# Two rounds of three chains in the first mixer of a two-block transformer kernel, with products in runs, and the modulation vectors computed in another stage

## The chip, the cores and the metric

The kernel runs on one core of a Trainium2 chip. The metric is the device time of one execution in microseconds (us), from runs on the chip. TensorE (PE in the profile) does the matrix products, VectorE (DVE), ScalarE (ACT) and GpSimd (POOL) the work on elements, and SyncE (SP) issues the transfers from memory. Each engine has one instruction queue, worked through in order.

## The reference

Two blocks follow each other, on one sequence of 256 positions with 1024 features, all in fp32.

```python
def first_block(x, p, ...):                 # two layers
    for i in range(2):
        h = rmsnorm(x, norm_mix_g[i])
        if i == 0:
            proj = h @ even_w_in[0]
            y_a = rwkv7_group(h, ...)        # 8 heads of 64: a recurrence over positions
            y_b = gdn_group(...)             # 4 heads of 128: the gated delta rule
            mix = concat(y_a, y_b) @ even_w_out[0]
        else:
            mix = chunk_band_attention(h, ...) @ attn_w_out[0]
        x = x + mix
        x = x + square(relu(rmsnorm(x) @ mlp_w1[i])) @ mlp_w2[i]
        x = x + rmsnorm(p[i] @ ple_w_proj[i]) * sigmoid(x @ ple_w_gate[i])
    return x

def second_block(x, c, ctx, c_ctx, w_ada, b_ada, ...):
    for layer in range(2):
        mod_l = silu(c) @ w_ada[layer] + b_ada[layer]      # w_ada[layer] is [1024, 6144]
        mod_c = silu(c_ctx) @ w_ada[layer] + b_ada[layer]
        # shifts, scales and gates of both streams come from mod_l and mod_c
        ...
```

## The kernel before

**Weights and products.** The activations lie with features on partitions, as eight tiles of 128 features by 256 positions. For fp32 accuracy each matrix product is done as three: weights and activations are split into a high and a low part. A weight piece [128, 1024] (512 KB, tile raw) is loaded by SP; ACT makes its high part (tile hi), and an engine named by `k.weng` makes the low part as raw - hi (tile lo); pools of four raw, three hi and three lo buffers hold them. `mm3` then issues the three products of a 128 x 128 block. Such products, 128 x 128 by 256 columns, are called dense below.

**The order.** The code is traced into instructions with a priority each, and a scheduler puts them in a fixed order per engine before the kernel runs. `k.at(p)` sets the priority of what is traced next (smaller is earlier), and `k.spread(p0, p1, n)` spreads the pieces of a dense chunk evenly over a stretch of priorities. The order is therefore decided by numbers in the code, not at run time.

**The first mixer** (`layer0_mixer`). The RWKV7 heads make four units and the gated delta rule (GDN) two; each unit is a chain of small steps for two heads: products of 64 x 64 or 128 x 64 on PE, each followed by DVE or ACT, which feed the next product. In both kinds there is the inverse of a triangular matrix by doubling (`triangular_inverse`: tiles Tt, Tg, Pg, Aa). Six units run in three rounds of two: RWKV units 0 and 1, RWKV units 2 and 3, GDN units 0 and 1. A round has `UNIT` = 320 priorities, both of its units start at the same one, and each unit has a lane: its own work buffers and two PSUM banks (`k.lane`, pools psX0 to psX2; psD is for dense products, psG for the modulation vectors). Between the small products stand dense ones, which need no unit: chunks 3, 1, 5 of the input projection w_ein in the first round, chunks 6, 8, 10, 7, 9, 11 and the gates of GDN (`gdn_gates`) in the second, chunks 12, 13, the RWKV half of the output projection (`out_proj1`) and the projection of the PLE gate (`ple[0].products`) in the third.

**The modulation vectors** of block 2's first layer (`ada`) are computed in the mixer too: a loop over 12 chunks of 512 columns, each with 4 pieces of 512 KB (tile adaraw) and 8 products of 32 result rows by 512 columns. Four column groups of PE (q = 0, 32, 64, 96) each take a quarter of the work; ACT copies the result (adat), four transposes and a sum on DVE bring it into place. The chunks lie `STEP` = 65 priorities apart. Those of the second layer are computed later in block 2, on DVE (`ada_sums`).

**What follows the mixer**: `out_proj`, the MLP of layer 0 (`mlp`, whose second half reads tile hh), the PLE gate, and `layer1_mixer`, the banded attention with its projection w_qkv, then the same again for layer 1, and block 2.

While the first mixer runs, `k.weng` is GpSimd; everywhere else, and in the mixer's first two chunks, it is DVE.

Of the kernel before, what the change touches and what calls it, by code (L numbers as in the profile page):

```python
# [19 lines left out]
P = 128  # L20
# [171 lines left out]
def layout(i):  # L192
# [22 lines left out]
    A["w_ada0"] = pack_w(i["w_ada_2"][0], 2, 512)  # L215
# [19 lines left out]
STEP = 65  # L235
F10 = 12
F20 = 7
# [3 lines left out]
OFS0 = 140  # L241
# [31 lines left out]
class K:  # L273
    def __init__(self, nc, tc, A, es):
        self.nc, self.tc, self.A, self.es = nc, tc, A, es
        self.cp = self.pool("const", 1)
        self.wraw = self.pool("wraw", 4)
        self.whi = self.pool("whi", 3)
        self.wlo = self.pool("wlo", 3)
        self.psG = self.pool("psG", 1, PSUM)  # L280
# [4 lines left out]
        self.weng = nc.vector  # L285
        self.slots = None
        self.later, self.slow = [], []
# [85 lines left out]
    def mm(self, out, lhsT, rhs, start=True, stop=True):  # L373
        self.nc.tensor.matmul(out=out, lhsT=lhsT, rhs=rhs, start=start, stop=stop)  # L374

    def tr(self, out, in_):
        self.nc.tensor.transpose(out=out, in_=in_, identity=self.ident)  # L377
# [410 lines left out]
def gdn_gates(k, gp, hgl, wbb, rb):  # L788
# [6 lines left out]
    ps = k.psX.tile([P, 2, T], F32, name="psx")  # L795
# [4 lines left out]
    ps = k.psX.tile([P, 2, 8], F32, name="psx")  # L800
# [18 lines left out]
    psn = k.psX.tile([P, 512], F32, name="psx")  # L819
# [151 lines left out]
def layer0_mixer(k, x, bg, ple):  # L971
# [5 lines left out]
    f1ps = [k.pool(f"f1{i}", n, es=es) for i, n in enumerate((F10, L1, L1))]  # L977
    f2ps = [k.pool(f"f2{i}", n, es=es) for i, n in enumerate((F20, L2, L2))]
# [10 lines left out]
    lanes = [lane(1), lane(2)]  # L989
# [72 lines left out]
    bg()  # L1062
    lo2 = []
    weng, k.weng = k.weng, nc.vector
# [3 lines left out]
    k.weng = weng  # L1068
# [47 lines left out]
    for q in range(3):  # L1116
        p = t0 + q * L
        if q == 0:
            dense((3, 1, 5), evac_rkv, p, p + L * 0.9)
        elif q == 1:  # L1120
            dense((6, 8, 10, 7, 9, 11), evac_gdn, p, p + L)
            k.at(p + L // 2)
            G = gdn_gates(k, gp, H, wbb, rb)
        else:
            dense((12, 13), evac_gdn, p, p + L * 0.5)
            yh, yl = y = k.acts(0)
            for m in range(4):
                k.split_act(yh[:, m, :T], yl[:, m, :T], ya[m])
            with k.spread(p + EO[0] * L, p + EO[1] * L, 16):
                for _ in out_proj1(k, "w_eout", y, x, [(0, 0, 4)]):  # L1130
                    pass
            k.at(p + PL * L)
            for _ in ple.products(lambda: k.psD.tile([P, 2, T], F32, name="psx")):
                pass
        for u in range(2):
            k.at(p + u * OFS)
            k.lane(1 + u)
            if q < 2:
                m = 2 * q + u
                ya.append(rwkv_unit(k, m, rkv[0, m], rkv[1, m], rkv[2, m], lt, lo2, rst, *lanes[u]))  # L1140
            else:
                yo.append(gdn_unit(k, u, G, [kq[2 * u], kq[2 * u + 1]], raws[1, u], raws[2, u], *lanes[u]))
            k.lane(0)
    k.at(t0 + 3 * L)
# [209 lines left out]
def layer1_mixer(k, xg, r, pass1):  # L1354
# [46 lines left out]
    pipe, groups = Pipe(), []  # L1401
    for g in range(4):
# [29 lines left out]
def ada(k, l, es, step, ofs=0):  # L1432
# [3 lines left out]
    w = k.pool("adaw", 2 if l else 3, es=es, side="right")  # L1436
# [8 lines left out]
    for c in range(12):  # L1445
        k.tc.cur_priority = p + step * c
        ps = k.psG.tile([P, 512], F32, name="psg")
        for pi in range(4):
            raw = w.tile([P, 2, 512], F32, name="adaraw")
            nc.sync.dma_start(out=raw, in_=k.A[f"w_ada{l}"][c, pi].rearrange("p (j n) -> p j n", j=2))  # L1450
            for j in range(2):
                kk = 2 * pi + j
                q = 32 * (kk % 4)
                nc.tensor.matmul(out=ps[q:q + 32], lhsT=sv[:, kk], rhs=raw[:, j], start=kk < 4, stop=kk >= 4, tile_position=(0, q))  # L1454
# [759 lines left out]
def program(nc, tc, A, out):  # L2214
    with ExitStack() as es:
# [4 lines left out]
        es1 = ExitStack()  # L2220
        k.plep = k.pool("plep", 1, es=es1, side="right")
        ple = [Ple(k, l) for l in range(2)]
        with ExitStack() as esa:
# [7 lines left out]
        for l in range(2):  # L2231
            st = k.stat_begin(stp, "ffn")
            xg = k.acts(1)
            out_proj(k, "w_eout" if l == 0 else "w_ao", y, x, f"gffn{l}", st, xg, [(1, 2, 2)] if l else [(1, 0, 4)])
# [7 lines left out]
            mlp(k, l, x, xg, st, xs, ple[l].norm, context if l else None)  # L2242
            if l == 0:
# [8 lines left out]
                y = layer1_mixer(k, nx, r, lambda y: chain(out_proj1(k, "w_ao", y, x, [(0, 0, 4), (1, 0, 2)]), ple[1].products(lambda: k.psD.tile([P, 2, T], F32, name="psx"))))  # L2252
# [23 lines left out]
```

## Time and profile before

| | us |
|---|---|
| median of 3 runs | 1981.81 |
| lowest and highest run | 1980.93, 1985.22 |
| the profiled execution, its own time | 1984.02 |
| its span, from the first to the last instruction | 1982.2 |
| PE busy in it | 1904.9 |
| DVE, ACT, POOL busy | 1382.6, 911.6, 161.3 |

The profiled execution is 2.2 us above the median, and 1.8 us of its time lie outside the span. Busy times are those of a hardware profiler; a matmul's end is modelled, and an fp32 matmul leaves two records where the instruction is one (for the small products and those of the modulation vectors). Of TensorE's clock the profile shows the granted share: 1.00 is 2.4 GHz and 0.50 is 1.2 GHz.

In time, the mixer's three rounds lie at about 68 to 175, 175 to 301 and 301 to 389 us; the first product of the second half of layer 0's MLP starts at 494.3 us; the attention lies at about 608 to 729 us.

### The profile page before, as it was taken

Reading aid. Unit: us, or ns where it says so; the run is one execution under the profiler, and the core shown is the slowest. Engines: PE = TensorE matmul, PEld = TensorE weight load, DVE = VectorE, ACT = ScalarE, POOL = GpSimd, SP = SyncE. Lnnn points to the kernel's source line nnn. Section 1 sums busy time; section 2 is a strip of 40 time slices with the busy share of each in tenths; the row PEclk is TensorE's granted clock in tenths of the full one; section 3 lists DMA queues with packets and bytes.
Section 4 is the critical chain, followed back from the end, with each engine's and each line's share of the span. In section 5 each row is a group of like instructions: output and inputs, shape, how many; then the busy total and the mean of one; then the engine's idle time right before and its main releaser. Section 6 shows DMA issues by size and latency. Waiting matters only on the chain.

```text
span 1982.2 us, 36281 instructions
## 1 busy us (share of the span) xinstructions
PE 1904.9 (96%) x14540; PEld 1682.0 (85%) x14540; DVE 1382.6 (70%) x2838; ACT 911.6 (46%) x1527; POOL 161.3 (8%) x211
## 2 busy tenths in 40 slices
PE   7999999999999999999999998899999999899998
PEld 4665668899999889999998887678888898788998
DVE  6544627586558878676876789859877578888664
ACT  4313224455446665545465555433213354465443
POOL 3412214100000100000001100000000000200000
PEclk9999978999999999999999999899999999999999
DMA  6544312255655446556422113235774254324553
GB/s 242 205 165 149 97 57 75 67 186 184 194 192 199 154 130 206 185 193 195 154 81 62 44 38 104 90 128 197 239 267 157 86 172 158 107 77 161 189 182 127
DMA packets 84401, 292.14 MB, mean 147 GB/s; under 512 B 9639, under 2 KB 11528, under 8 KB 83976
## 3 DMA queue, kind: packets, MB, share of 16 engines
q1 hardware_dynamic: 84232, 289.82, 44.3%
q8 instruction: 114, 1.87, 0.4%
q14 instruction: 55, 0.45, 0.1%
HBM read 288.73 MB, written 1.05 MB: 146 GB/s over the span
## 4 chain that ended last, share of the span: by engine, by line
PE 81%; DVE 13%; ACT 2%; issue 2%; POOL 1%; DMA 0%; ACTq 0%; SPq 0%; DVEq 0%
PE psx L374 75%; PE psg L1454 3%; DVE lo L364 3%; PE psx L377 2%; PE psg L374 1%; ACT hi L361 1%; POOL qb L364 1%; DVE mt L371 1%; DVE act L371 0%; DVE qx L364 0%; DVE hu L371 0%; ACT act L361 0%; DVE qms L1309 0%; DVE act L364 0%; DVE nt L364 0%
## 5 line engine op out<-in xcount | busy, mean ns | idle before, releaser
L374 PE MATMUL psx<-act,hi 128*128 128x256 f32 (+1 forms) x3872 | 830.2, 309 | 23.4 <-ACT hi L361 11.4
L361 ACT ACTIVATE hi<-raw 128x1024 fp32r<-128x1024 f32 (+1 forms) x440 | 453.6, 1032 | 652.0 <-PE psx L374 459.1
L374 PEld LDWEIGHTS psx<-act,hi 128*128 128x128 f32 x3872 | 633.9, 192 | 92.3 <-issue 32.4
L364 DVE TENSOR_TENSOR lo<-raw,hi 128x1024 fp32r<-128x1024 f32 (+1 forms) x406 | 482.0, 1189 | 265.8 <-ACT hi L361 264.2
L374 PE MATMUL psx<-act,lo 128*128 128x256 f32 (+1 forms) x1936 | 596.4, 308 | 4.1 <-DVE lo L364 3.6
L374 PEld LDWEIGHTS psx<-act,lo 128*128 128x128 f32 x1936 | 371.7, 192 | 42.1 <-issue 18.8
L374 PE MATMUL psx<-hi,act 128*128 128x256 f32 x1280 | 242.2, 289 | 2.7 <-ACT act L361 1.5
L374 PEld LDWEIGHTS psx<-hi,act 128*128 128x128 f32 x1280 | 198.8, 190 | 11.2 <-issue 7.0
L374 PE MATMUL psx<-lo,act 128*128 128x256 f32 x640 | 180.8, 283 | 1.2 <-DVE lo L364 1.2
L374 PE MATMUL psx<-fh,hi 128*128 128x256 f32 (+2 forms) x528 | 162.3, 308 | 4.9 <-DVE xc L371 4.9
L374 PE MATMUL psx<-fh,lo 128*128 128x256 f32 (+2 forms) x528 | 162.4, 308 | 1.3 <-DVE lo L364 1.3
L374 PE MATMUL psx<-fl,hi 128*128 128x256 f32 (+2 forms) x528 | 161.7, 306 | 0.0
L374 PE MATMUL psx<-hh,hi 128*128 128x256 f32 x512 | 142.4, 278 | 0.0
L374 PE MATMUL psx<-hlo,hi 128*128 128x256 f32 x512 | 142.2, 278 | 0.0
L374 PE MATMUL psx<-hh,lo 128*128 128x256 f32 x512 | 142.2, 278 | 0.0
L374 PEld LDWEIGHTS psx<-lo,act 128*128 128x128 f32 x640 | 121.5, 190 | 1.4 <-DVE lo L364 1.4
L374 PEld LDWEIGHTS psx<-fh,hi 128*128 128x128 f32 x528 | 101.3, 192 | 10.9 <-issue 6.0
L374 PEld LDWEIGHTS psx<-fh,lo 128*128 128x128 f32 x528 | 101.3, 192 | 8.0 <-DVE lo L364 2.1
L374 PEld LDWEIGHTS psx<-fl,hi 128*128 128x128 f32 x528 | 101.3, 192 | 4.5
L364 POOL TENSOR_TENSOR lo<-raw,hi 128x1024 fp32r<-128x1024 f32 x34 | 81.4, 2396 | 223.6 <-ACT hi L361 167.7
L1484 DVE CUSTOM_DVE_ANT_0 adat<-adaraw,adac 128x1024 f32<-128x1024 f32 x64 | 78.3, 1223 | 28.1 <-DMA adaraw<-in_w_ada 27.1
L374 PEld LDWEIGHTS psx<-hlo,hi 128*128 128x128 f32 x512 | 96.9, 189 | 0.0
(499 smaller groups left out, 2501.6 us busy)
## 6 DMA issues: line engine op xcount, KB each, us to landing
raw<-in_w_m SPq DMA_DIRECT2D x128, 512.0 KB, 3.4
adaraw<-in_w_ada SPq DMA_DIRECT2D x96, 512.0 KB, 4.2
raw<-in_w_up SPq DMA_DIRECT2D x92, 512.0 KB, 3.3
raw<-in_w_dn SPq DMA_DIRECT2D x48, 512.0 KB, 3.4
raw<-in_w_ein SPq DMA_DIRECT2D x28, 512.0 KB, 4.7
raw<-in_w_ie SPq DMA_DIRECT2D x28, 512.0 KB, 3.4
raw<-in_w_qkv SPq DMA_DIRECT2D x24, 512.0 KB, 3.5
raw<-in_w_io SPq DMA_DIRECT2D x18, 512.0 KB, 3.7
```

What stands on the lines that cost most here:

```text
L361: self.nc.scalar.activation(out=out, in_=in_, func=func, **kw)
L364: (eng or self.nc.vector).tensor_tensor(out=out, in0=a, in1=b, op=op)
L371: (eng or self.nc.vector).scalar_tensor_tensor(out=out, in0=a, scalar=s, in1=b, op0=op0, op1=op1)
L374: self.nc.tensor.matmul(out=out, lhsT=lhsT, rhs=rhs, start=start, stop=stop)
L377: self.nc.tensor.transpose(out=out, in_=in_, identity=self.ident)
L1454: nc.tensor.matmul(out=ps[q:q + 32], lhsT=sv[:, kk], rhs=raw[:, j], start=kk < 4, stop=kk >= 4, tile_position=(0, q))
L1484: nc.vector.tensor_tensor_reduce(out=t, in0=raw, in1=row[:, s], scale=1.0, scalar=0.0, op0=ALU.mult, op1=ALU.add, accum_out=mod[:, j, s:s ...
```

## The change

The six units run in two rounds of three (RWKV 0, 1, 2; then RWKV 3, GDN 0, 1), with a third lane of buffers and banks; psG, the bank of the modulation vectors, is opened after the mixer only. Chunks 3, 1, 5 stand in the first quarter of the first round, then the gates (with their products in the dense banks psD), then chunks 6 to 11. The products that a unit traces directly behind each other are kept together (`k.chains`, `k.pe`): the first of such a run keeps its priority, the others get priority 0 with the condition to be issued after the first. `ada` is called in the attention, with 2 pieces of 1 MB a chunk, each with four products in a run, and `STEP` = 120. The low part of a weight is made by DVE everywhere. The PLE projection of layer 0 stands in its MLP, and the fourth piece of the output projection's RWKV half in `out_proj`.

```diff
-STEP = 65
+STEP = 120
-F20 = 7
+F20 = 10
-OFS0 = 140
+OFS0 = 100
...
-        self.nc.tensor.matmul(out=out, lhsT=lhsT, rhs=rhs, start=start, stop=stop)
+        self.pe(lambda: self.nc.tensor.matmul(out=out, lhsT=lhsT, rhs=rhs, start=start, stop=stop))
...
+    def pe(self, emit):
+
+        if not self.runs:
+            emit()
+            return
+        traced = self.nc.cur_bb.bb.instructions
+        if self.head is not None and traced[-1] is self.last:
+            p = self.now
+            self.at(0)
+            with self.tc.issue_after(self.head):
+                self.last = emit().ins
+            self.at(p)
+        else:
+            self.head = self.last = emit().ins
...
-        self.tt(lo[:, :n], raw[:, :n], hi[:, :n].bitcast(F32), ALU.subtract, eng=self.weng)
+        self.tt(lo[:, :n], raw[:, :n], hi[:, :n].bitcast(F32), ALU.subtract)
...
-    ps = k.psX.tile([P, 2, T], F32, name="psx")
+    ps = k.psD.tile([P, 2, T], F32, name="psx")
...
-    k.banks(2, 1, 2, 2)
+    k.banks(2, 2, 2, 2)
...
-    for q in range(3):
+    rwkv = lambda u, m: ya.append(rwkv_unit(k, m, rkv[0, m], rkv[1, m], rkv[2, m], lt, lo2, rst, *lanes[u]))
+    gdn = lambda u, i: yo.append(gdn_unit(k, i, G, [kq[2 * i], kq[2 * i + 1]], raws[1, i], raws[2, i], *lanes[u]))
+    for q in range(2):
         p = t0 + q * L
         if q == 0:
-            dense((3, 1, 5), evac_rkv, p, p + L * 0.9)
-        elif q == 1:
-            dense((6, 8, 10, 7, 9, 11), evac_gdn, p, p + L)
-            k.at(p + L // 2)
+            dense((3, 1, 5), evac_rkv, p, p + L * 0.25)
+            k.at(p + L * 0.25)
             G = gdn_gates(k, gp, H, wbb, rb)
+            dense((6, 8, 10, 7, 9, 11), evac_gdn, p + L * 0.25, p + L)
+            units = [(rwkv, 0), (rwkv, 1), (rwkv, 2)]
         else:
             dense((12, 13), evac_gdn, p, p + L * 0.5)
...
-                for _ in out_proj1(k, "w_eout", y, x, [(0, 0, 4)]):
+                for _ in out_proj1(k, "w_eout", y, x, [(0, 0, 3)]):
                     pass
-            k.at(p + PL * L)
-            for _ in ple.products(lambda: k.psD.tile([P, 2, T], F32, name="psx")):
-                pass
-        for u in range(2):
+            units = [(rwkv, 3), (gdn, 0), (gdn, 1)]
+        for u, (f, i) in enumerate(units):
             k.at(p + u * OFS)
-            k.lane(1 + u)
...
+            k.lane(u)
+            with k.chains():
+                f(u, i)
...
-        for pi in range(4):
-            raw = w.tile([P, 2, 512], F32, name="adaraw")
...
+        for pi in range(2):
+            raw = w.tile([P, 4, 512], F32, name="adaraw")
+            nc.sync.dma_start(out=raw, in_=k.A[f"w_ada{l}"][c, pi].rearrange("p (j n) -> p j n", j=4))
+
+            with k.chains():
+                for j in range(4):
+                    q = 32 * j
+                    k.pe(lambda: nc.tensor.matmul(out=ps[q:q + 32], lhsT=sv[:, 4 * pi + j], rhs=raw[:, j], start=pi == 0, stop=pi == 1, tile_position=(0, q)))
...
-            k.weng = nc.gpsimd
-            y = layer0_mixer(k, x, lambda: ada(k, 0, esa, STEP, OFS0), ple[0])
-            k.weng = nc.vector
...
+                y = layer1_mixer(k, nx, r, lambda y: chain(out_proj1(k, "w_ao", y, x, [(0, 0, 4), (1, 0, 2)]), ple[1].products(space)), lambda: ada(k, 0, esm, STEP, OFS0))
```

The order of PE before, in the first inverse of the first round (each row is a run of equal instructions; Tg, Aa, Pg, Tt are the inverse's tiles, adaraw and sv the modulation's weights and vector, act with hi or lo a dense product):

```order
L374 MATMUL psx<-Tg,Aa 64x64 x16
L1454 MATMUL psg<-adaraw,sv 32x512
L374 MATMUL psx<-Pg,Tt 64x64 x16
L1454 MATMUL psg<-adaraw,sv 32x512 x4
L374 MATMUL psx<-Tg,Aa 64x64 x16
L1454 MATMUL psg<-adaraw,sv 32x512
L374 MATMUL psx<-act,lo 128x256
L374 MATMUL psx<-act,hi 128x256 x2
L374 MATMUL psx<-act,lo 128x256
L374 MATMUL psx<-Pg,Tt 64x64 x16
```

Two units' steps take turns there with modulation products, alone or in fours, and with single dense ones. The same place after (bbrow belongs to the gates):

```order
L373 MATMUL psx<-tm,Aa 64x64 x24
L822 MATMUL psx<-ct,bbrow 128x8 x2
L373 MATMUL psx<-Tg,Aa 64x64 x24
L373 MATMUL psx<-Pg,Tt 64x64 x24
...
L373 MATMUL psx<-Tt,Pg 64x64 x24
L373 MATMUL psx<-Tt,tm 64x64 x24
L373 MATMUL psx<-Z,Tt 64x64 x24
L373 MATMUL psx<-tm 128x128
```

Each step is now a run of 24 products of three units, and nothing else stands between the steps: the dense products of chunks 6 to 11 come behind the inverse. PE after, in the attention, where before there are dense products alone (hi and lo with act are those of w_qkv, adat the copied result that is transposed):

```order
L373 MATMUL psx<-hi,act 128x256 x2
L1471 MATMUL psg<-adaraw,sv 32x512 x4
L373 MATMUL psx<-lo,act 128x256
L373 MATMUL psx<-hi,act 128x256
L1471 MATMUL psg<-adaraw,sv 32x512 x4
L373 MATMUL psx<-hi,act 128x256
L373 MATMUL psx<-lo,act 128x256
...
L376 MATMUL psg<-ct,adat 128x128 x4
```

All modulation products have moved there, in 24 groups of four (three chunks have both of their groups behind each other), with twelve groups of four transposes. Behind the MLP of layer 1 the order of PE is the same in both kernels.

## Rows read from the trace of the kernel before

**Rows 1.** The page: span, and PE's busy time, share and instructions.
```profile
span 1982.2 us, 36281 instructions
PE 1904.9 (96%) x14540; PEld 1682.0 (85%) x14540; DVE 1382.6 (70%) x2838; ACT 911.6 (46%) x1527; POOL 161.3 (8%) x211
```

**Rows 2.** Windows: stretch, length, each engine's busy time, clock, DMA share, GB/s.
```profile
0.00:494.30 494.30, 465.53 (x3994) 359.46 (x3995) 286.04 (x610) 193.93 (x321) 106.08 (x86) 0.95 0.42 143
68.00:175.00 107.00, 100.29 (x944) 65.12 (x947) 56.11 (x149) 30.30 (x63) 24.57 (x22) 0.97 0.47 161
175.00:301.00 126.00, 122.01 (x976) 78.58 (x968) 57.79 (x167) 38.30 (x77) 23.98 (x19) 0.87 0.29 95
301.00:389.00 88.00, 83.50 (x906) 75.32 (x904) 57.94 (x147) 39.46 (x67) 31.25 (x21) 0.95 0.21 67
414.50:494.30 79.80, 79.80 (x674) 79.78 (x673) 57.63 (x74) 43.84 (x57) 0.00 (x0) 1.00 0.57 188
608.00:729.00 121.00, 118.25 (x993) 110.06 (x992) 92.54 (x293) 74.50 (x164) 8.64 (x4) 0.99 0.47 155
```

**Rows 3.** PE's groups by operation, 0 to 389 us: busy, mean ns, idle before.
```profile
L374 PE MATMUL psx<-act,hi 128*128 128x256 f32 x576 | 134.7, 315 | 12.1 <-ACT hi L361 10.9 <-DVE zsh L364 1.2
...
L1454 PE MATMUL psg<-adaraw,sv 128*32 128x512 f32 x192 | 76.2, 616 | 1.9 <-DMA adaraw<-in_w_ada 1.9
...
L377 PE MATMUL psg<-ct,adat 128*128 128x128 f32 x48 | 9.0, 295 | 0.0
```

**Rows 4.** PE's timeline from 60 us: start, duration, instruction.
```profile
60.54 0.28 PE L374 MATMUL psx<-act,lo 128*128 128x256 f32 x1
60.65 0.28 PE L374 MATMUL psx<-act,hi 128*128 128x256 f32 x1
60.87 1.05 PE L1454 MATMUL psg<-adaraw,sv 128*32 128x512 f32 x4
61.85 0.39 PE L374 MATMUL psx<-act,hi 128*128 128x256 f32 x1
62.07 0.28 PE L374 MATMUL psx<-act,lo 128*128 128x256 f32 x1
```

**Rows 5.** PE's timeline from 113 us, in the first inverse.
```profile
113.34 1.04 PE L1454 MATMUL psg<-adaraw,sv 128*32 128x512 f32 x2
114.32 1.20 PE L374 MATMUL psx<-Pg,Tt 64*64 64x64 f32 x32
115.45 1.06 PE L1454 MATMUL psg<-adaraw,sv 128*32 128x512 f32 x8
```

**Rows 6.** Windows of five stretches at the low clock, 104 to 323 us.
```profile
104.40:111.30 6.90, 6.90 (x52) 5.69 (x51) 1.11 (x5) 1.26 (x3) 0.00 (x0) 0.51 0.45 167
...
248.20:272.10 23.90, 23.90 (x84) 16.24 (x84) 5.09 (x21) 9.04 (x17) 2.43 (x2) 0.51 0.13 45
...
sum 47.80, PE 47.41 PEld 34.35 DVE 13.60 ACT 14.64 POOL 5.60; mean PE 9.48 PEld 6.87 DVE 2.72 ACT 2.93 POOL 1.12
```

**Rows 7.** ACT's and DVE's timeline in the same inverse.
```profile
113.41 0.66 ACT L361 ACTIVATE Pg<-psx 128x256 f32<-128x256 f32 x2
115.52 0.79 DVE L619 COPY_PREDICATED Tg<-cm,psx 128x256 f32<-128x256 uint32 x2 [5.49 <-PE psx L374]
116.19 0.76 DVE L634 STREAM_TRANSPOSE Tt<-Tg 128x256 f32<-128x256 f32 x2
```

**Rows 8.** Window of a stage in block 2, columns as in Rows 2.
```profile
1200.00:1300.00 100.00, 84.81 (x463) 71.14 (x462) 85.14 (x207) 50.11 (x101) 0.78 (x10) 0.88 0.29 95
```

**Rows 9.** Groups of POOL and DVE up to 480 us: the low parts.
```profile
L364 POOL TENSOR_TENSOR lo<-raw,hi 128x1024 fp32r<-128x1024 f32 x34 | 81.4, 2396 | 223.6 <-ACT hi L361 167.7 <-PE psx L374 29.4 <-ACT Pg L361 26.4
...
L364 DVE TENSOR_TENSOR lo<-raw,hi 128x1024 fp32r<-128x1024 f32 x35 | 42.7, 1223 | 19.0 <-ACT hi L361 18.8
```

**Rows 10.** The page: transfer rate in 40 slices, and the main queue's MB and share.
```profile
GB/s 242 205 165 149 97 57 75 67 186 184 194 192 199 154 130 206 185 193 195 154 81 62 44 38 104 90 128 197 239 267 157 86 172 158 107 77 161 189 182 127
...
q1 hardware_dynamic: 84232, 289.82, 44.3%
```

More of the change, by code (lines that the diff above doesn't have):

```diff
@@ L284, in __init__ @@
         self.pse = None
-        self.weng = nc.vector
         self.slots = None
+        self.runs, self.head = False, None
         self.later, self.slow = [], []
@@ L373, in mm, with chains @@
     def mm(self, out, lhsT, rhs, start=True, stop=True):
-        self.nc.tensor.matmul(out=out, lhsT=lhsT, rhs=rhs, start=start, stop=stop)
+        self.pe(lambda: self.nc.tensor.matmul(out=out, lhsT=lhsT, rhs=rhs, start=start, stop=stop))
     def tr(self, out, in_):
-        self.nc.tensor.transpose(out=out, in_=in_, identity=self.ident)
+        self.pe(lambda: self.nc.tensor.transpose(out=out, in_=in_, identity=self.ident))
+    def pe(self, emit):
[11 more added lines that the diff above has]
+            self.head = self.last = emit().ins
+    @contextmanager
+    def chains(self):
+        self.runs = True
+        yield
+        self.runs, self.head = False, None
     def vec(self, name, j=0, n=1):
@@ L988, in layer0_mixer @@
     f1, f2, f4 = lane(0)
-    lanes = [lane(1), lane(2)]
+    lanes = [lane(i) for i in (1, 2, 3)]
     hh, hl_ = k.acts(0)
@@ L1435, in ada @@
     nc = k.nc
-    w = k.pool("adaw", 2 if l else 3, es=es, side="right")
+    w = k.pool("adaw", 2, es=es, side="right")
     o = k.pool("adao", 1, es=es, side="right")
@@ L1447, in ada @@
         ps = k.psG.tile([P, 512], F32, name="psg")
-        for pi in range(4):
-            raw = w.tile([P, 2, 512], F32, name="adaraw")
[L1450 to L1454, printed above, removed]
+        for pi in range(2):
[5 more added lines that the diff above has]
+                    k.pe(lambda: nc.tensor.matmul(out=ps[q:q + 32], lhsT=sv[:, 4 * pi + j], rhs=raw[:, j], start=pi == 0, stop=pi == 1, tile_position=(0, q)))
         t = o.tile([P, 512], F32, name="adat")
@@ L2220, in program @@
         es1 = ExitStack()
+        y = layer0_mixer(k, x)
         k.plep = k.pool("plep", 1, es=es1, side="right")
         ple = [Ple(k, l) for l in range(2)]
-        with ExitStack() as esa:
-            k.weng = nc.gpsimd
-            y = layer0_mixer(k, x, lambda: ada(k, 0, esa, STEP, OFS0), ple[0])
-            k.weng = nc.vector
+        space = lambda: k.psD.tile([P, 2, T], F32, name="psx")
+        k.pse.close()
+        k.pse = None
+        k.psG = k.pool("psG", 1, PSUM)
         k.banks(3, 4)
@@ L2233, in program @@
             xg = k.acts(1)
-            out_proj(k, "w_eout" if l == 0 else "w_ao", y, x, f"gffn{l}", st, xg, [(1, 2, 2)] if l else [(1, 0, 4)])
+            out_proj(k, "w_eout" if l == 0 else "w_ao", y, x, f"gffn{l}", st, xg, [(1, 2, 2)] if l else [(0, 3, 1), (1, 0, 4)])
             xs = k.acts(0)
@@ L2240, in context, with first @@
                 ctx.extend([hc, k.trickle(context_start(k, hc), NPACE5)])
-            mlp(k, l, x, xg, st, xs, ple[l].norm, context if l else None)
+            def first():
+                if l == 0:
+                    for _ in ple[0].products(space):
+                        pass
+                ple[l].norm()
+            mlp(k, l, x, xg, st, xs, first, context if l else None)
             if l == 0:
@@ L2251, in program @@
                 r = k.stat_rstd(st, D, EPS)
-                y = layer1_mixer(k, nx, r, lambda y: chain(out_proj1(k, "w_ao", y, x, [(0, 0, 4), (1, 0, 2)]), ple[1].products(lambda: k.psD.tile([P, 2, T], F32, name="psx"))))
+                esm = ExitStack()
+                y = layer1_mixer(k, nx, r, lambda y: chain(out_proj1(k, "w_ao", y, x, [(0, 0, 4), (1, 0, 2)]), ple[1].products(space)), lambda: ada(k, 0, esm, STEP, OFS0))
+                esm.close()
             else:
```

31 lines of the change are left out of this document (12 added, 19 removed).

## The prediction, made before the changed kernel was run

> **What bounds the kernel now.** I read the page's head first: TensorE (PE) is busy 1904.9 of 1982.2 us [rows 1], so only PE's own time, or waits of PE, can move the end. The windows by stage come next [rows 2]. Up to 494.3 us (the first w_m2 product of layer 0, which stands in both orders at the same place of the program) PE is busy 465.5 of 494.3 us at a clock of 0.95; the three rounds of the mixer take 107, 126 and 88 us with 6.7, 4.0 and 4.5 us of idle (15.2 together); and a purely dense stretch has 674 products in 79.80 us, all busy, so 0.118 us for a dense product. The reader should see that the mixer is no latency problem before: PE is full there. What fills it, the groups by operation show [rows 3]: the modulation products of block 2 (adaraw) take 76.2 us in 192 records, that is 96 matmuls (two records each), and PE idles 12.1 us for the dense products, mostly for ACT's hi. The timelines say why they are dear: two of them (four records) take 0.98 us (60.87 to 61.85) [rows 4], a single one takes as long (113.34 to 114.32), and four behind each other have 1.06 us where the single one has 1.04 [rows 5], for the four go to four column groups and lie over each other. The order of before has them in 69 runs, 51 of them single.
>
> The same timeline prices a change of kind on PE: dense product to dense product 0.11 us, dense to adaraw 0.22, and adaraw to dense leaves 0.22 before the next [rows 4], so about 0.10 us a change. Counted in the orders up to the common point, the kinds (dense, modulation, small) change 386 times before and 126 times after. Last, the clock: in five stretches of the rounds, 47.8 us together, it is 0.5, the lower of its two levels (1.2 and 2.4 GHz) [rows 6]; at the upper one the same work would take 24 us less.
>
> So before, up to 494.3: 1776 dense products x 0.118 = 210, modulation 76, its transposes 6, changes 386 x 0.10 = 39, half clock 24, idle 29 (15 of it in the rounds, 14 ahead of and between them); what is left, about 110 us, are the small products of the chains, the same in both kernels.
>
> **The change, part by part.**
>
> *Modulation out of the mixer.* 76.2 us go. The 12 groups of four transposes went through PE beside them: 48 in 9.0 us busy [rows 3], 0.75 a group, of which the modelled end of the last lies beside what follows, as a dense product's 0.28 lie over the next ones' 0.11 [rows 4]; I take 0.5, 6 us. No PE work replaces them there.
>
> *Products in runs.* 260 fewer changes x 0.10 = 26 us. This rests on the scheduler having made the runs, and the order after shows them (24 products of three chains behind each other where before 16 of two stood with modulation and dense products between).
>
> *Three chains in two rounds.* The products are the same, so their sum is too. What is lost is cover: in the first round the dense chunks 6 to 11 come behind the inverse, whose steps follow each other with nothing between. One step there: 16 small products take 1.13 us start to start [rows 5], so 24 take 1.7; behind them ACT's copy of a pair takes 0.66 us, DVE's masked copy 0.79 and its transpose 0.76 [rows 7]. The chains' steps follow each other on every engine, so while DVE works for one chain, PE has the two others; I count 0.6 us of wait for each of about ten steps in two rounds, 12 to 13 us more idle. Below: nothing more than the 15.2 us of now, if the three chains cover each other. Above: a stage with little dense work further on, 1200 to 1300 us, where PE idles 15 of 100 us [rows 8]; the two rounds last some 200 us without the dense run between them, so 30 us more, and with 15 us for gates that hold dense products up (a rival below) 45. I take 13, nearest to a step of this very chain. The half clock I leave at 24 us; it could go altogether (a gain of 24) since the interleaving that went with it is gone.
>
> The mixer's side: 76 + 6 + 26 - 13 = 95 us less, so the first w_m2 product at about 399 us (bounds 60 to 132 less).
>
> *lo on DVE alone.* 34 pieces that took 2.40 us on POOL would take 1.22 on DVE [rows 9], 41 us more. DVE is busy 286 of 494 us now [rows 2]; with 327 of 399 it comes to 82%. A stage where it has 92.5 of 121 us, 76%, leaves PE full [rows 2]; one with 85% has PE idle for 15% [rows 8]. I take it as hidden: whi and wlo have three buffers each, so a piece may be made while two others are used. Without that cover each late lo costs PE up to 1.2 us, 34 x 1.2 = 41 us, which is the same idle as in the bound above.
>
> *Modulation in the attention.* 24 pieces of 1 MB, each with a run of four: 0.98 us and 0.2 for two changes = 1.18, x 24 = 28 us (three of the chunks have both runs together, nothing changes by it); transposes 12 x 0.6 = 7. PE is busy 118.3 of 121 us there [rows 2], so all 35 us are added. ACT copies and DVE sums of twelve chunks are hidden: ACT is at 74.5, DVE at 92.5 of 121 us; 2 us for a late one.
> The transfers: the stage moves 155 GB/s x 121 us = 19 MB now; 25 MB come to it, 44 MB in 121 + 35 = 156 us, 282 GB/s. The queue's whole traffic took 44.3% of the span for 289.82 MB, 330 GB/s while it moves, and the busiest slice of the page had 267 [rows 10]. At 330 it fits, at 267 it needs 165 us, 9 us more. A dense weight of 512 KB that queues behind one piece comes 3 us late; with eight such 25 us. I take 7, nearer the busiest slice, and 0 and 25 as ends. Together +44 us (35 to 60).
>
> *PLE products and three of four pieces of w_eout.* The same dense products at another place: nothing; they lie in stretches where PE is full [rows 2] and would cost at most their first weight's 3 us if unprefetched.
>
> Sum: 1984.0 (the profiled execution) - 95 + 44 = 1933. It is 2.2 us above the median of before, so **1931 us** in its terms, 2.6% less.
>
> **The rivals.** All prices are against 1931. No-difference means within 0.2% (4 us).
>
> *A, the other side: the clock falls in the chains.* With no dense products between the small ones, the rounds run at the lower clock. In the trace the fall goes with stretches of scattered small products: 248.2 to 272.1 has 84 products in 23.90 us, clock 0.51 [rows 6]. Of the 110 us of small products all would double, less about 30 hidden in waits that are there anyway: +80, 2011 us. It decides from 50 us of loss on, that is when about 100 us more than now are at half clock. Against it: the inverse at 113 to 117 us ran at the full clock (0.98 us for its modulation products too [rows 5]), and dense runs stand on both sides. Chance 0.06.
> The Trainium skill ("TensorE: Matmul & The Clock Gate", the section "HAM oscillation — how this bites in real kernels") lays the half clock on idle gaps of PE between bursts, and the chains of the change make such gaps, where before modulation filled them: by the page it speaks against this change. The row of 248.2 to 272.1 differs: PE was busy all its 23.90 us.
>
> *B, the attention waits for transfers.* Sustained rates stay at the 267 GB/s of the busiest slice or lower, and dense weights queue behind 1 MB pieces: +18 over what I took, 1949 us. For it: PE waited for adaraw only 1.9 us in the mixer [rows 3], but there the rate was 95 to 161 GB/s [rows 2]. Chance 0.2.
>
> *C, the chains' latency is bare.* Three chains do not cover each other, and the gates' products, which take the dense products' banks, hold up chunks 6 to 11, or DVE, at 82%, is late with lo: idle +45 in place of 13, 1963 us. For it: the order after has no dense product within the first inverse, and [rows 8]. Chance 0.15.
>
> *D, better than the sum.* The half clock goes with the interleaving and the chains cover each other: 24 + 13 us less, 1894; half of it, 1912. For it: of 465 us of PE work only 333 are needed (210 + 110 + 13). Chance 0.17.
>
> *E, it does little:* modulation in the attention is not packed, 96 x 0.98 = 94 + 7 us instead of 35, and the net is about nothing, 1990. Against it the order, with fours in a row on four column groups. Chance 0.02.
>
> **How the numbers follow.** The forecast's own case holds 0.40 and spans 1918 to 1942. The range reaches up over B and most of C and down over most of D: 1900 to 1966, leaving out A, E and the tails of C and D, 0.18 in all. Slower by over 0.2%: A and the half of E, 0.07; within 0.2%: the other half of E, and B and C at once (1981 us), 0.03; faster: the rest, 0.90.
>
> **What the profile after would show.** Right: first w_m2 product near 399 us; no adaraw before 400 us; changes of 24 small products with idle of about 0.6 us a step; dense runs at 0.118; in the attention 24 runs of four with 0.98 us each, PE still full, the stage some 40 us longer. Wrong: clock 0.5 over much of the two rounds (A); PE idle for DMA of raw or adaraw in the attention (B); PE idle above 45 us before the common point, for DVE or ACT (C); rounds together under 190 us (D). What would upset all of it is a dense stretch behind layer 0's mixer that changes though its order is the same.

## The result, and the profile after

The changed kernel takes 1907.21 us (median of 4 runs, 1903.15 to 1910.38), against 1981.37 (4 runs, 1977.54 to 1985.22): a ratio of 0.9614 with a 95% interval of 0.9578 to 0.9650, or 74 us less. 1931 was forecast, in a range of 1900 to 1966.

The head of the page, and windows of the changed kernel (columns as in [rows 2]): up to its first w_m2 product at 379.1 us, the first round, the dense stretch between the rounds, the second round, the w_m2 products of layer 0, the stretch from there to those of layer 1, and within it the one with the modulation.

```profile
span 1905.5 us, 36257 instructions
PE 1832.2 (96%) x14540; PEld 1668.0 (88%) x14540; DVE 1384.2 (73%) x2878; ACT 909.3 (48%) x1527; POOL 72.4 (4%) x175
```

```profile
0.00:379.10 379.10, 351.15 (x3755) 326.90 (x3756) 279.99 (x624) 185.32 (x309) 20.59 (x50) 0.96 0.37 123
48.80:142.70 93.90, 88.90 (x1230) 77.70 (x1229) 66.32 (x205) 39.33 (x83) 7.91 (x16) 0.96 0.17 58
142.70:170.70 28.00, 28.00 (x233) 27.82 (x232) 26.86 (x53) 15.92 (x24) 1.33 (x5) 1.00 0.45 147
170.70:262.90 92.20, 84.49 (x1108) 73.59 (x1107) 68.14 (x205) 40.86 (x80) 10.34 (x14) 0.93 0.12 39
379.10:471.00 91.90, 91.90 (x768) 91.90 (x767) 46.30 (x44) 36.84 (x37) 0.00 (x0) 1.00 0.56 184
471.00:751.00 280.00, 276.21 (x2277) 244.22 (x2276) 200.04 (x450) 159.40 (x283) 5.17 (x4) 1.00 0.68 240
504.00:651.00 147.00, 143.86 (x1184) 113.10 (x1182) 97.58 (x306) 80.32 (x175) 5.17 (x4) 1.00 0.74 272
```

The span is 76.7 us shorter. The common point stands at 379.1 instead of 494.3 us [rows 2], 115.2 us earlier, and behind it 38.5 us are lost again (1526.4 instead of 1487.9 us). PE is still the bound: 28.0 us idle up to the common point, 28.8 before. The clock there is 0.96 after 0.95: since it has two levels, 2 x 0.04 x 379 = 30 us at the lower one, before 49 by the same sum.

PE's timeline in the first inverse of the changed kernel; two records are one product, so x48 are the 24 of a run:

```profile
92.66 2.39 PE L373 MATMUL psx<-Tg,Aa 64*64 64x64 f32 x48 [1.82 <-DVE Tg L645]
94.84 2.38 PE L373 MATMUL psx<-Pg,Tt 64*64 64x64 f32 x48
97.05 1.74 PE L373 MATMUL psx<-Tg,Aa 64*64 64x64 f32 x48
98.63 0.63 PE L373 MATMUL psx<-Pg,Tt 64*64 64x64 f32 x16
99.96 1.15 PE L373 MATMUL psx<-Pg,Tt 64*64 64x64 f32 x32 [0.70 <-ACT Pg L360]
100.94 1.85 PE L373 MATMUL psx<-Tg,Aa 64*64 64x64 f32 x48
102.63 1.57 PE L373 MATMUL psx<-Pg,Tt 64*64 64x64 f32 x48
104.03 1.74 PE L373 MATMUL psx<-Tg,Aa 64*64 64x64 f32 x48
```

The waits in brackets are what the three chains leave uncovered: 1.82 us ahead of the first of these steps and 0.70 us once behind it. From 97.05 us on a step takes 1.4 to 1.7 us for three chains, waits aside, where two took 1.13 [rows 5] with a modulation product of 0.98 behind it. The first two steps take 2.2 us each, for they stand at the lower clock, behind a stretch in which PE was busy less than half of the time:

```profile
89.80:93.20 3.40, 1.57 (x45) 1.42 (x43) 3.40 (x12) 1.07 (x3) 0.00 (x0) 1.00 0.02 5
93.20:96.60 3.40, 3.40 (x72) 3.40 (x68) 0.75 (x5) 3.17 (x7) 0.00 (x0) 0.50 0.00 0
```

And in the attention, first some of PE's timeline, then all its waits from 471 to 751 us:

```profile
541.98 1.06 PE L1471 MATMUL psg<-adaraw,sv 128*32 128x512 f32 x8
542.98 0.39 PE L373 MATMUL psx<-lo,act 128*128 128x256 f32 x1
543.20 0.28 PE L373 MATMUL psx<-hi,act 128*128 128x256 f32 x1
543.41 1.07 PE L1471 MATMUL psg<-adaraw,sv 128*32 128x512 f32 x8
```

```profile
PE psg L376 <- ACT adat L360: 2.2, 2, 1.3
PE psx L373 <- DVE act L370: 0.7, 2, 0.4
PE psx L373 <- DVE Q L363: 0.6, 1, 0.6
```

Four modulation products take 1.00 us from start to start there, where 0.98 was forecast, and no wait is for a transfer. Twice PE waits for ACT's copy of a result, 2.2 us together.

### The profile page after: what moved, and what is told of

Read it like the earlier page. It is cut to its first block, busy times and chain, and to the rows that moved or that the text cites. A ratio compares the mean times of both kernels' runs of the same rounds, so it can differ in the third digit from the quotient of the medians.

```text
span 1905.5 us, 36257 instructions
## 1 busy us (share of the span) xinstructions
PE 1832.2 (96%) x14540; PEld 1668.0 (88%) x14540; DVE 1384.2 (73%) x2878; ACT 909.3 (48%) x1527; POOL 72.4 (4%) x175
## 4 chain that ended last, share of the span: by engine, by line
PE 57%; DVE 7%; ACT 1%; issue 1%; POOL 1%; ACTq 0%; DVEq 0%
PE psx L373 54%; DVE lo L363 2%; PE psx L376 2%; PE psg L373 1%; POOL qb L363 1%; DVE mt L370 0%; DVE act L370 0%; ACT hi L360 0%; DVE qx L363 0%; PE psg L1471 0%; DVE hu L370 0%; DVE act L363 0%; DVE qms L1323 0%; DVE qtmp L363 0%; POOL hYb L363 0%
## 5 line engine op out<-in xcount | busy, mean ns | idle before, releaser
L373 PE MATMUL psx<-act,hi 128*128 128x256 f32 (+1 forms) x3872 | 815.3, 307 | 23.8 <-ACT hi L360 12.1
L363 DVE TENSOR_TENSOR lo<-raw,hi 128x1024 fp32r<-128x1024 f32 (+1 forms) x444 | 526.4, 1187 | 296.9 <-ACT hi L360 295.5
L373 PEld LDWEIGHTS psx<-hh,lo 128*128 128x128 f32 x512 | 97.1, 190 | 0.0
L373 PEld LDWEIGHTS psx<-hh,hi 128*128 128x128 f32 x512 | 96.6, 189 | 0.0
```

Source lines behind the costliest of these rows:

```text
L363: (eng or self.nc.vector).tensor_tensor(out=out, in0=a, in1=b, op=op)
L373: self.pe(lambda: self.nc.tensor.matmul(out=out, lhsT=lhsT, rhs=rhs, start=start, stop=stop))
```

## The experiments

Each ratio is against before, by runs on the same chip, with its 95% interval; the clock and idle columns are of the stretch up to the first w_m2 product in the profile. The runs come from several chips, on which the median of before was 1980.0 to 1984.4 us, so a difference of medians is good to some 4 us. The clock has two decimals, so the times at the lower level worked out from it are good to about 4 us too.

| kernel | median us | ratio | first w_m2 at | PE idle | clock |
|---|---|---|---|---|---|
| before | 1981.4 | 1 | 494.3 | 28.8 | 0.95 |
| before, modulation moved | 1964.3 | 0.9909 (0.9878-0.9939) | 448.8 | 51.2 | 0.89 |
| before, no modulation | 1933.4 | 0.9749 (0.9704-0.9793) | 450.9 | 54.7 | 0.88 |
| before, runs | 1963.3 | 0.9910 (0.9877-0.9944) | 472.2 | 31.4 | 0.98 |
| before, lows on DVE | 1955.2 | 0.9857 (0.9820-0.9894) | 465.4 | 23.8 | 0.99 |
| before, moved and runs | 1954.5 | 0.9849 (0.9812-0.9886) | 436.3 | 47.4 | 0.91 |
| changed, three rounds of two | 1910.4 | 0.9642 (0.9615-0.9669) | 393.5 | 25.2 | 0.96 |
| changed | 1907.2 | 0.9614 (0.9578-0.9650) | 379.1 | 28.0 | 0.96 |
| changed, no modulation | 1877.6 | 0.9471 (0.9441-0.9501) | 377.4 | 30.1 | 0.98 |
| changed, no runs | 1985.1 | 1.0008 (0.9982-1.0035) | 455.1 | 32.0 | 0.89 |
| changed, lows on GpSimd | 1934.4 | 0.9761 (0.9727-0.9796) | 400.5 | 38.0 | 0.94 |

**The modulation moved, alone.** `ada` as in the change, called in the attention; all else as before.

```diff
-            y = layer0_mixer(k, x, lambda: ada(k, 0, esa, STEP, OFS0), ple[0])
+            y = layer0_mixer(k, x, lambda: None, ple[0])
...
```

> The kernel before with one part of the change alone: the modulation vectors are computed in the attention, in runs of four; rounds, chains, GpSimd's lows stay. Theory 1 (PE's own time: 69 runs of modulation products in the mixer at 0.98 us and two changes of kind, 0.2, each, and 7 us of transposes = 88 us, against some 33 us in the attention): about 55 us faster, 1926 us, that is three quarters of the change's 74. Theory 2 (the two rounds of three chains and the runs are what gains, the modulation only changes its place): within 15 us of before, 1966 to 1985. Theory 3 (taken out of two-chain rounds, the modulation leaves the chains' waits bare): 20 to 35 us faster, with PE idle in the three rounds up from 15 to 35 us or more.

17 us: by the time alone between the second and the third of the three theories, nearer the second. But its window shows another thing:

```profile
0.00:448.80 448.80, 397.59 (x3754) 359.77 (x3755) 290.75 (x584) 191.67 (x311) 109.51 (x85) 0.89 0.30 99
```

The modulation's PE time did go, and came back as two other things. Idle rose by 22 us (51.2 instead of 28.8), and at a clock of 0.89, 2 x 0.11 x 449 = 99 us ran at the lower level instead of 49, which costs 25 us. PE's waits in the same stretch, the four largest, and then the two largest of before up to 494.3 us:

```profile
PE psx L375 <- ACT hi L362: 10.7, 1, 10.7
PE psx L378 <- DVE nrs L372: 9.1, 3, 4.2
PE psx L378 <- DVE ors L372: 5.9, 1, 5.9
PE psx L375 <- DVE gtn L372: 5.0, 1, 5.0
```

```profile
PE psx L374 <- ACT hi L361: 11.4, 2, 10.9
PE psx L377 <- DVE nrs L371: 4.6, 3, 1.9
```

The first is the kernel's start, the others are steps on DVE (a row's rsqrt and its like). In before the same nrs costs half as much, and ors and gtn are not among the waits: the modulation had filled that time. Theory 3 had that mechanism, but only half of it: the clock came on top.

**No modulation in before.** The call of `ada` is replaced by a constant, so its products, transposes and loads are left out.

```diff
-            y = layer0_mixer(k, x, lambda: ada(k, 0, esa, STEP, OFS0), ple[0])
+            y = layer0_mixer(k, x, lambda: nc.vector.memset(k.mods[0], 0.25), ple[0])
```

> The kernel before without the modulation vectors of block 2's first layer: their products, transposes and loads are left out and the vectors are a constant. Prices the modulation in the mixer. Theory 1: 88 to 100 us less (88 of PE time, and a part of the 24 us of half clock), 1881 to 1893 us. Theory 3 (waits of the chains come out from under it): 50 to 65 us less, 1916 to 1931. Against the run with the modulation moved, the difference is what the modulation costs in the attention: 31 to 35 us by theory 1.

48 us less, not 88: with the modulation gone altogether the mixer is as slow as with it moved (450.9 and 448.8 us). So in before the modulation cost about half of its PE time, a little less even than theory 3 had it. The 31 us between this run and the one before it are its price in the attention.

**No modulation in the changed kernel.**

```diff
-... lambda: ada(k, 0, esm, STEP, OFS0))
+... lambda: nc.vector.memset(k.mods[0], 0.25))
```

> The changed kernel without the modulation vectors of block 2's first layer (products, transposes and loads left out, the vectors are a constant). Prices them in the attention. Theory 1 (PE time alone): 24 runs at 1.18 us and 12 groups of transposes at 0.5 to 0.6 = 34 to 35 us less, 1872 us. Rival (25 MB of loads and ACT's copies cost waits beyond that): 45 to 60 us less, 1847 to 1862. Rival (a part was hidden in waits of the attention): under 27 us.

30 us between the medians, and the stage between the w_m2 products of the two layers is 32 us longer with the modulation (280.0 against 247.7 us): PE's time alone and a little less than reckoned. The loads cost nothing: the window 504 to 651 us above has 272 GB/s over 147 us, with PE busy 143.9 us, and none of the waits above is for a transfer.

**No runs in the changed kernel's mixer.** The modulation keeps its fours.

```diff
-            with k.chains():
-                f(u, i)
+            f(u, i)
```

> The changed kernel without the runs in the mixer: the products of the units keep their own priorities (the modulation keeps its runs of four). The order then has 246 changes of kind up to the first w_m2 product instead of 127. Theory 1 (0.10 us a change): 12 us slower, 1919 us. Rival (the runs decide the rounds, since scattered products bring the low clock and make each step late): 30 us or more slower. Rival (the single products fit into waits anyway): within 4 us of 1907.

The kernel is back at the time of before, 78 us slower, for the same products on PE in another order. PE idles hardly more (32.0 against 28.0 us). Two windows and, of the first, some of PE's timeline:

```profile
139.00:145.90 6.90, 6.90 (x66) 5.13 (x63) 3.33 (x7) 1.06 (x1) 0.00 (x0) 1.00 0.01 2
145.90:193.60 47.70, 47.70 (x257) 36.71 (x257) 11.33 (x29) 6.89 (x18) 0.14 (x2) 0.50 0.09 26
```

```profile
140.80 0.33 PE L373 MATMUL psx<-Pg,Tt 64*64 64x64 f32 x4
141.06 0.39 PE L373 MATMUL psx<-act,hi 128*128 128x256 f32 x1
141.38 0.44 PE L373 MATMUL psx<-Pg,Tt 64*64 64x64 f32 x4
141.75 0.39 PE L373 MATMUL psx<-act,lo 128*128 128x256 f32 x1
```

PE is busy 6.90 of 6.90 us there, with a few small products (two, most often) and a dense one by turns, and for the next 47.70 us it runs at the lower clock, busy throughout. In the changed kernel the dense stretch from 142.7 to 170.7 us has 233 products at 1.00. From 379.1 to 455.1 us is 76 us: 2 x 0.11 x 455 = 100 us at the lower level instead of 30 cost 35 of them, idle 4, and the rest, some 37, is the dearer order itself (a turn of two small products and a dense one takes 0.58 us, 140.80 to 141.38; within a run a small product takes 0.07, a dense one 0.12, 0.26 together), which 119 more changes at 0.10 us would have made 12. By this turn, with two changes and 0.32 us more than in runs, they make some 19; where the rest of the 37 arises is not shown.

**Runs in before, alone.** `pe` and `chains` as in the change, around the two units of each round.

```diff
+            with k.chains():
+                if q < 2:
...
```

> The kernel before with one part of the change alone: the units' products are kept in runs on PE; three rounds of two chains, the modulation in the mixer and GpSimd's lows stay. Theory 4 (products scattered one by one bring the low clock and cost more each; runs take that away, with any number of chains): the low-clock time before the first w_m2 product falls from 48 us to under 30, small products go from 0.061 us to 0.057, some 15 us faster by clock and 10 by price: 1950 to 1960 us. Rival 5 (the single modulation products between the steps keep the order broken, and the clock up, whatever the runs): within 8 us of before, with about as much low clock as before.

18 us, all ahead of the common point, and the clock there is 0.98 in place of 0.95, so 19 us at the lower level instead of 49. Theory 4 has the direction and the clock, but not the price: counted over the trace without the half clock, a record of a small product takes 0.060 us from start to start in both kernels. PE is busy 25 us less; what the clock does not explain of it, some 9 us, goes with about 80 fewer changes of kind in the trace, 0.11 us each.

**Lows on DVE, in before, alone, and on GpSimd in the changed kernel.** The first is one line; the second brings `k.weng` back as in before.

```diff
-            k.weng = nc.gpsimd
+            k.weng = nc.vector
```

> The kernel before with the lows of the mixer made by DVE instead of GpSimd, nothing else. In the changed kernel this part was worth 27 us. If it acts through the speed of the lows and of DVE's own steps beside GpSimd: 10 to 27 us faster, 1955 to 1972. If PE, full with the modulation, covers it in before: within 5 us of before.

> The changed kernel with the lows of the mixer made by GpSimd again. Theory as predicted (DVE's 41 us more are hidden, a low on GpSimd takes 2.4 us instead of 1.2 and comes later, DVE's own steps beside it are slower): 0 to 12 us slower, 1907 to 1919. Rival (DVE at over 70% holds the chains up, so taking work off it helps): 5 to 15 us faster.

The largest of the three parts that were added to before alone: 26 us by the medians, and 27 when it is taken out of the changed kernel. DVE's groups up to 480 us, first before, then with all lows on DVE (36 and 12 operations of the same shape in each):

```profile
L371 DVE SCALAR_TENSOR_TENSOR dsh<-zsh,vt,dsh 128x256 f32<-128x256 f32 x36 | 17.9, 533 | 0.2
L368 DVE TENSOR_SCALAR dsh<-zsh,vt 128x256 f32<-128x256 f32 x12 | 10.2, 879 | 0.3
L364 DVE TENSOR_TENSOR dsh<-zsh 128x512 f32<-128x512 f32 x6 | 7.2, 1192 | 0.4
```

```profile
0.00:465.40 465.40, 441.62 (x3995) 346.47 (x3996) 283.31 (x646) 195.62 (x322) 20.88 (x50) 0.99 0.44 152
```

```profile
L371 DVE SCALAR_TENSOR_TENSOR dsh<-zsh,vt,dsh 128x256 f32<-128x256 f32 x36 | 16.2, 476 | 0.1
L368 DVE TENSOR_SCALAR dsh<-zsh,vt 128x256 f32<-128x256 f32 x12 | 4.5, 387 | 0.0
L364 DVE TENSOR_TENSOR dsh<-zsh 128x512 f32<-128x512 f32 x6 | 4.1, 689 | 0.3
```

A TENSOR_SCALAR takes 387 ns on average where it took 879 beside GpSimd. The two means hide what happens: with the fastest, the median and the slowest of the twelve, in ns, first before, then with all lows on DVE, and below them such an operation, the next of its kind and the low on GpSimd at that time, in before:

```profile
L368 DVE TENSOR_SCALAR dsh<-zsh,vt x12: 340/352/2448, 182.4 to 311.5; 128x256 f32<-128x256 f32 x12
L368 DVE TENSOR_SCALAR dsh<-zsh,vt x12: 338/346/831, 174.0 to 275.3; 128x256 f32<-128x256 f32 x12
```

```profile
182.38 1.64 DVE L368 TENSOR_SCALAR dsh<-zsh,vt 128x256 f32<-128x256 f32 x1
184.01 0.34 DVE L368 TENSOR_SCALAR dsh<-zsh,vt 128x256 f32<-128x256 f32 x1
181.49 2.38 POOL L364 TENSOR_TENSOR lo<-raw,hi 128x1024 fp32r<-128x1024 f32 x1 [8.02 <-ACT hi L361]
```

The medians are alike. A few operations, begun while GpSimd made a low, ended only just behind it (184.02 and 183.87 us here), and the next one had its usual time. Counted over the trace of before, 24 DVE operations ahead of the common point overlap a low on GpSimd and take over 0.3 us more than the median of their kind, some 40 us together; with the lows on DVE only 3 such long ones are left, 2 us. So DVE, with 34 more lows, is busy 283.3 us up to the common point where it was busy 286.0: the 41 us were given back in full. Late lows were not the cost in before: PE waited for one from GpSimd 0.4 us in all. On PE the gain shows as idle 5 us less and a clock of 0.99: 13.7 us stand at the lower level (281.0 to 284.4 and 352.6 to 362.9 us) instead of 48, worth 17; the rest of the 29 us at the common point, some 7, is not traced, nor are the steps from held-up operations to the clock. In the changed kernel with GpSimd the same two move back: 10 us idle, and 48 us at the lower level instead of 30, 9 more.

**Moved and runs, in before.**

> The kernel before with two parts of the change: the modulation in the attention and the units' products in runs; three rounds of two chains and GpSimd's lows stay. Alone the first gave 16 us and the second 21. Theory 4 (the modulation's place pays only once the runs keep the clock up): more than the sum, 45 us or more faster, 1935 or less, with low clock before the first w_m2 product at 50 us or less, where the modulation moved alone had 102. If the parts only add: 1944.

27 us by the medians of the table, 30 by the ratio: not more than the sum of the two, and the lower clock did not go (0.91), so theory 4 as put there falls. Runs alone don't keep the clock up once the modulation is out, with GpSimd still at the lows: idle is 47.4 us, nearly that of the moved modulation alone. PE's largest wait behind the kernel's start is for nrs on DVE, 10.6 us; for lows from GpSimd it waits 2.6 us.

**Three rounds of two in the changed kernel.** The dense chunks as in before; all else as changed, so this is the run before plus DVE's lows (and the moved PLE products and fourth piece, the gates in psD and more buffers, none of which was run alone).

```diff
-    for q in range(2):
+    for q in range(3):
...
+            dense((3, 1, 5), evac_rkv, p, p + L * 0.9)
+            units = [(rwkv, 0), (rwkv, 1)]
```

> The changed kernel with three rounds of two chains, the dense chunks spread as before; runs, DVE's lows and the modulation in the attention stay. Theory 4 (the runs are what keeps the clock; how many chains stand together matters little): 1907 to 1922 us. Rival 6 (three chains cover each other's DVE and ACT steps, two don't once the modulation is gone, as the idle of the run with the modulation moved, 40 us against 17, suggests): 1930 to 1950 us, with PE idle up by 20 us or more.

71 of the 74 us without the third chain; the intervals of the two overlap, so the 3 us are not shown. 44 us come from the step from the run before to this one, where the lows alone were worth 26. At the common point they are idle, 22 us less, and half clock (0.96 in place of 0.91), some 24 less. The third lane brings the common point forward by 14 us (393.5 to 379.1; in the run with two, 12 modulation products and four transposes stand ahead of it, some 4 us of these). Of this 8 are lost in the w_m2 products of both layers, which is the next question.

**The price of a w_m2 product.** The same 768 products, busy throughout at the full clock, took 86.70 us in before and in the run with two chains, and 91.90 us in the changed kernel. First the window of the run with two chains, then of the changed kernel with 64 bytes of padding ahead of hh, then with every dense operand placed at multiples of 128 bytes (this one also with a longer row of act):

```profile
393.50:480.20 86.70, 86.70 (x767) 86.70 (x766) 46.27 (x44) 37.00 (x37) 0.00 (x0) 1.00 0.57 195
```

```profile
378.70:470.00 91.30, 91.30 (x778) 91.30 (x777) 46.95 (x45) 37.67 (x38) 0.00 (x0) 1.00 0.56 186
```

```profile
377.80:470.00 92.20, 92.20 (x771) 92.20 (x770) 46.29 (x44) 36.79 (x37) 0.00 (x0) 1.00 0.55 183
```

Three runs belong to it. The scratch area of the change, in before:

```diff
-    nc = bacc.Bacc("TRN2", target_bir_lowering=False, num_devices=1)
+    nc = bacc.Bacc("TRN2", target_bir_lowering=False, num_devices=1, dynamic_dma_scratch_size=1024)
```

> The kernel before with the program's argument for the DMA scratch area set to 1024 as in the change, nothing else: all buffers lie at other addresses. A w_m2 product takes 0.115 us from start to start in all kernels made from before (duration 276 ns) and 0.119 to 0.122 in all made from the changed one (284 ns). If the place of the buffers sets it: 284 ns, and 7 to 9 us slower, 1988 us. If it is something else (the moved PLE buffers, the order): 276 ns and no difference.

> The changed kernel with 64 unused bytes a partition ahead of the MLP's buffers, so that hh and hlo begin at a multiple of 128 bytes (107392 instead of 107328), as they do in before (122496), in the run with two chains (107136) and in the one with the scratch area changed (107136), which all have 113 ns from one w_m2 product to the next, where those with 107328 have 120. If the address decides: 113 ns, 2 x 768 products x 6.5 ns = 10 us less in both MLPs, 1897 us. If it is something else that goes with the changed kernel: 120 ns, 1907.

> The changed kernel with hh and hlo as in the run beside this one, and every other moving operand of the dense products at multiples of 128 bytes: the low and high weights begin 64 bytes later, and a row of the activations' tile act takes 288 words instead of 258 (1152 bytes instead of 1032). If the address decides there too, some 6,000 more products go from 118 or 119 ns to 113: 30 to 36 us less than the run with hh alone, about 1863 us. If those products are held by something else (evacuation, weights loaded): within 6 us of the run with hh alone.

The scratch area alone: 1988.4 us, ratio 1.0022 (0.9994 to 1.0049), and 86.70 us for the products: no cause. With hh at 107392, 1902.6 us, ratio 0.9581 (0.9551 to 0.9612), and 91.30 us for 778 records (ten of them others; the 768 take 118 ns each from start to start); with all operands placed, 1906.5 us, 0.9604 (0.9576 to 0.9631), and 120 ns. Neither is 113 ns: hh at a multiple of 128 bytes is not what decides, and the other products did not become cheaper. The interval of the first overlaps that of the changed kernel, so its 5 us are not shown to be a gain. Nor is the address of hh all of it: before, with hh at one place for both layers, pays 113 ns in layer 0 and 117 in layer 1 (829.9 to 919.6 us).

## Why the prediction was right, point by point

**What bounds it.** Right: PE before and after, 96% busy.

**The mixer's side: 95 us forecast, 115 measured (bounds 60 to 132).** As an account of PE the sum came out. PE was busy 465.5 us up to the common point and is busy 351.2: 114 us less, 10 of them by the clock, so some 104 of PE's own work, where 76 + 6 + 26 = 108 was forecast. The 20 us by which the forecast fell short are the idle that did not come (13) and the half clock that fell (10), less these 4. That the idle did not come is in part luck: with the lows on GpSimd the changed kernel does idle 9 us more than before (38.0 against 28.8), near the 13 of the forecast, and the lows on DVE, priced at nothing, took these away. As prices of the parts, three terms were wrong:

- *Modulation out of the mixer, 76 + 6 us (and its share of the changes, 14).* Its PE time was that, but what it was worth in before was 48 us, for two covers went with it: 22 to 26 us of idle, and 25 us and more of half clock. The step that failed is "what fills PE is what PE gains when it goes": in a stretch of small chained steps the filler hides waits, and it held the clock up. Only with the other parts did the whole of its PE time come out as a gain.
- *Products in runs, 26 us by 260 changes at 0.10.* As a term between the two orders it holds (104 - 82 = 22). As what the runs are worth it is mis-sized: without them the changed kernel loses 78 us, 35 of it by the clock. The change of kind was priced at the full clock, between dense and modulation products; a turn of two small products and a dense one, with its two changes, costs 0.3 us more than the same in runs.
- *lo on DVE alone, nothing.* The step that failed most plainly: 26 to 27 us gained, in both contexts. The 41 us were added to a DVE total that held some 40 us of operations held up by GpSimd's lows; DVE's total went down instead, by 2.7 us. The view that would have told it was in the trace before: one shape of DVE operation with durations far apart (340 to 2448 ns), according to whether GpSimd was at a low.
- *Three chains in two rounds, 13 us more idle.* None came (28.0 against 28.8). The chains cover each other, as the lower bound had it. The third chain itself is worth the 10 us that the common point moved; 3 us of the time as things lie, which the intervals don't show.
- *Half clock, left at 24 us.* Some 14 to 15 by the window.

**The attention: 44 us forecast, 30 measured.** The 35 us of PE time were near (the stage grew by 31 to 32 us). The 7 for transfers were not there; the 2 for ACT were, as 2.2 us of wait, but other waits of the stage fell as much (PE idles 3.8 us from 471 to 751 us, and 4.7 in before from 581 to 830). The other 8 us behind the common point (5 in layer 0's w_m2 products, 3 in layer 1's) were nobody's term: the text took work whose order is the same to cost the same, and named that as what would upset it.

**The rivals.** A, the falling clock, is real as a mechanism and came only in small part, some 27 to 30 us at the lower level; without the runs it was 100. Its place was for the most part wrong: the inverse without dense products ran at the full clock but for its first two steps (93.20 to 96.60 us above), and in the run without runs it was dense products and small ones by turns that were followed by 47.7 us at half clock. The rule of the Trainium skill ("TensorE: Matmul & The Clock Gate", "HAM oscillation — how this bites in real kernels") that gaps of PE bring the lower clock has a case here too. With the modulation moved alone:

```profile
145.90:152.70 6.80, 2.57 (x22) 2.34 (x21) 6.80 (x18) 1.43 (x2) 3.92 (x2) 1.00 0.37 117
152.70:166.30 13.60, 13.60 (x43) 8.26 (x42) 5.70 (x14) 8.70 (x13) 1.55 (x3) 0.50 0.05 19
```

PE was busy 2.57 of 6.80 us, waiting for DVE, and then the clock was 0.50. The trace agrees with that rule here, and in the changed kernel's inverse; the rows of 139 to 193.6 us above show that it is not the only way. Against the rule the prediction held the low stretch of 248.2 to 272.1 us in before, in which PE was busy; what bears on the rule is the stretch ahead of that one, and there PE was busy throughout too:

```profile
241.00:247.80 6.80, 6.80 (x100) 5.01 (x99) 1.19 (x3) 3.54 (x8) 1.87 (x1) 1.00 0.00 0
```

What exactly the clock answers to in a busy PE is not settled by these runs. B fell (272 GB/s sustained, no wait for it), C fell (idle did not rise), and D is what happened in part: its sign, rounds under 190 us together, came (93.9 + 92.2 = 186.1 us), and of its 37 us the median shows 24.

**Not tried.** The modulation in runs of four in the mixer of before, and DVE's lows with the moved modulation but without the runs; so how the last 44 us of the step to three rounds of two divide between the lows and what they make possible for the others is open. So is what sets the price of a w_m2 product.

## What to carry to other kernels

Work that fills PE between the steps of a chain can be worth less than its busy time when it is taken out (here 48 us of the 88 reckoned): ask what waits come out from under it, and what the clock does without it, and price both before the gain. Keep equal small products behind each other; scattered among dense ones they cost more here than their changes, for a stretch of such turns was followed by half clock with PE never idle. And when work is moved from one engine to another, look whether one holds the other up: operations of one shape, most of them fast and a few as long as the other engine's, say so, and a mean hides it.

## What was not expected of the hardware

- DVE beside GpSimd: the same TENSOR_SCALAR of 128x256 took 352 ns in the median with the lows on GpSimd and 346 without, but up to 2448 where it began beside a low, and it ended just behind that low; a low took 2396 ns on GpSimd and 1222 on DVE.
- The clock: 0.50 for 47.7 us after 6.9 us in which PE was fully busy with small and dense products by turns.
- A dense product's price differs between kernels whose buffers lie at other places: a w_m2 product of layer 0 took 113 ns with hh at 122496 or 107136 bytes of a partition, 118 at 107392, 120 at 107328 or 111360, at the full clock, with PE always busy. 64 bytes of padding alone took it from 120 to 118; what makes the rest was not found.
